# A hybrid decoder layer on one core: decode scores packed by sample, block scores in one product, values by mixed rows and triangles, and norm sums by 128 tokens

## The chip, the core and the metric

The kernel is one program on one core of a Trainium2 chip. Its engines work side by side, each through its own instructions in order: PE (TensorE, matrix products, with PEld for its weight loads), DVE (VectorE), ACT (ScalarE), POOL (GpSimd), and SP, which issues most transfers. Products go into one of eight banks of PSUM, each 512 float32 columns on 128 partitions, and DVE or ACT take them out from there. The metric is the device time of one execution in microseconds, the median of several runs.

## The reference

One step of a decoder layer in float32, for 1024 prompt tokens and 8 samples of 4 new tokens each (1056 tokens in all), width 1024. Cut to what the change touches:

```python
def _rms(x, g):
    y = xf * lax.rsqrt(jnp.mean(xf * xf, axis=-1, keepdims=True) + EPS)
    return y * g

def _sink_attention(q, k, v, mask, sinks):      # 8 heads of 64, 2 kv heads
    s = jnp.einsum('bnqhgd,bnkhd->bnhgqk', q, k) * (HEAD_DIM ** -0.5)
    s = jnp.where(mask, s, -jnp.inf)
    m = jnp.maximum(jnp.max(s, -1, keepdims=True), sink)
    p = jnp.exp(s - m)
    w = p / (jnp.sum(p, -1, keepdims=True) + jnp.exp(sink - m))
    return jnp.einsum('bnhgqk,bnkhd->bnqhgd', w, v)

def _layer(x, p, attn_fn, ...):
    h = _rms(x, n_mix_pre); z = h @ w_in         # q | k | v | u
    a = attn_fn(q, k, v)                         # prompt or sample
    m = pool_mixer(u)
    x = x + _rms(concatenate([a, m]) @ w_out, n_mix_post)
    f = _rms(x, n_ffn_pre)
    f = (silu(f @ w_gate) * (f @ w_up)) @ w_down
    x = x + _rms(f, n_ffn_post)
    return x + sigmoid(x @ w_ple_gate) * (p @ w_ple)
```

A prompt query attends to the 128 keys that end with its own: in blocks of 128 tokens these are the keys of its own block up to its place, and the keys of the block before it behind its place. A sample's query attends to the last 128 of 128 cached and 4 new keys of its own sample.

## The kernel before

**Tiling.** Activations lie with the width on partitions and tokens on columns, in three groups `g` of 352 tokens. Products of weights are made of two float32r halves of each operand (`wh`/`wl`, `mh`/`ml`, `fh`/`fl`): `gemm` issues three matmuls for each pair. ACT makes the high half by a copy and DVE the low half by a subtraction (`split`, lines 164 and 165). Attention's products (line 126, operands `a`), the transposes (line 120) and the norms' column sums are plain float32; one such product of float32 leaves two records in the trace, a transpose leaves one.

**Norms.** `rstd_steps` is a generator that the twelve norms of the kernel go through. The squares of a group stand in `acc`; four matmuls with `ones` give the sums of four times 88 tokens on 88 partitions, ACT and DVE take the root and its reciprocal (`sd`), split into two parts (`hl`). DVE multiplies each part into a diagonal (`dg`, two tiles of 88x352), and two matmuls with `ones_r` spread these over all partitions. A `yield` hands back to whatever is interleaved with the norm.

**Attention, decode.** `qd` holds the queries of 8 samples x 4 tokens x 4 heads, 128 in all, one kv head on each half of the partitions. `dscores(kv)` multiplies all of them with the keys of all samples (1024 cached and 32 new columns) and adds a mask that leaves each query its own sample's keys; `softmax` runs over 1056 columns, `dturned` transposes nine pieces, `dvalues` multiplies with the cached and new values.

**Attention, prompt.** The blocks run in the order 5, 6, 7, 0, 1, 2, 3, 4. `scores(b)` makes four heads x two kv heads x (own block, block before) products of 128 columns. ACT copies the part of the block before (line 678), DVE overwrites it with the own block's where the mask says so (line 679): a query's row then holds exactly its 128 keys. `softmax` reduces (DVE), exponentiates each head (ACT, line 642) and normalises (POOL, line 648). `turned` transposes the eight heads' weights; DVE multiplies each with two masks (lines 695 and 697), one result for the own block, one for the block before. `values` multiplies both with the values of the two blocks into one bank, and `put` splits the result into `mixa` (ACT line 627, DVE line 628).

**Order.** In this part PE's order is pinned to the order of the code. `filler(n)` takes the next output products (`out_pool`, `out_attn`, `out_proj`) from a list and puts them between the attention steps, so that PE has work while softmax and masks run on the others; what is left is issued behind the last block. The order on the other engines, outside what is pinned, comes from a scheduler. Tiles of activations share one pool with `A_SLOTS` places; a transfer into such a tile waits until its place is free.

Of the kernel before, what the change touches and what calls it, by code (L numbers as in the profile page):

```python
# [10 lines left out]
F32 = mybir.dt.float32  # L11
# [5 lines left out]
P = 128  # L17
D = 1024
# [11 lines left out]

TB = 4
WIN = 128
# [24 lines left out]

A_SLOTS = 27


@with_exitstack
def trunk_kernel(
# [61 lines left out]
    def mm(*args, **kw):  # L124

        ins = te.matmul(*args, **kw)  # L126
        if pinned[0]:
            tc.keep_in_program_order(ins)
# [4 lines left out]
    def tmp(n, s="t", dt=F32):  # L133
        return spool.tile([P, n], dt, tag="tmp", bufs=6, name=nm(s), padded_shape=[P, NX])
# [172 lines left out]
    def rstd_steps(acc):  # L307

        n = acc.shape[1]
        w = n // TB
# [4 lines left out]
        se.activation(sd[:w], sm[:w, :TB], AF.Sqrt, bias=epst[:w], scale=1.0 / D)  # L317
        ve.reciprocal(sd[:w], sd[:w])
        hl = spool.tile([P, 2, TB], F32R, tag="hl", name=nm("hl"))
        ve.tensor_copy(hl[:w, 0], sd[:w])  # L320
        ve.tensor_tensor(hl[:w, 1], sd[:w], hl[:w, 0].bitcast(F32), op=ALU.subtract)
        dgs = []
        for h in range(2):
            dg = tmp(n, "dg", F32R)
            ve.tensor_tensor(
                dg[:w].rearrange("p (i k) -> p i k", k=w),
                ident[:w, :w].unsqueeze(1).to_broadcast([w, TB, w]),
                hl[:w, h].bitcast(F32).unsqueeze(2).to_broadcast([w, TB, w]),
                op=ALU.mult,
            )  # L330
            dgs.append(dg)
# [229 lines left out]
    def u_mix(c):  # L561

        for g in range(G):
# [27 lines left out]
    misc = act_tile([P, 6, P])  # L591
    qd, am, vdec = misc[:, 0, :], misc[:, 1:5, :], misc[: NDEC * DSEQ, 5, :]
    for c in range(4):
        n = NDEC * DSEQ
        ge.tensor_copy(qd[:, c * n : (c + 1) * n], qT[c][:, SEQ:])
    ys = [[half(g, s="y"), None] for g in range(G)]
# [4 lines left out]

    vtok = act_tile([P, NB, P])
    for h in range(2):
        ps = bank()
        for i in range(4):
            b = 4 * h + i
            te.transpose(ps[:, i * P : (i + 1) * P], vT[:, b * P : (b + 1) * P], ident)
        se.copy(vtok[:, 4 * h : 4 * h + 4, :], ps.rearrange("p (b c) -> p b c", c=P))
    ps = bank()
# [39 lines left out]

    def m4(i):  # L650
        return am[:, i, :].unsqueeze(1).to_broadcast([P, 4, WIN])

# [3 lines left out]
    def scores(b):  # L656


        t = act_tile([P, 8, WIN])
        cur = [bank() for _ in range(2)]  # L660
        prv = [bank() for _ in range(2)] if b else None
        for c in range(4):
            for which, at in ((cur, b), (prv, b - 1)):
                if which is None:
                    continue
                for kv in range(2):
                    rows = slice(64 * kv, 64 * kv + 64)
                    mm(
                        which[kv][:, c * WIN : (c + 1) * WIN],
                        qT[c][rows, b * WIN : (b + 1) * WIN],  # L670
                        kT[rows, at * WIN : (at + 1) * WIN],
                        start=True,
                        stop=True,
                    )
        for kv in range(2):
            tk = t[:, 4 * kv : 4 * kv + 4, :]
            if b:
                se.copy(tk, v4(prv[kv]))
                ve.copy_predicated(tk, m4(0).bitcast(mybir.dt.int32), v4(cur[kv]))
            else:  # L680
                ve.tensor_tensor(tk, v4(cur[kv]), m4(1), op=ALU.add)
            hs = slice(4 * kv, 4 * kv + 4)
            softmax(tk, 4, 0.125, skp[:, hs], nskp[:, hs])
        return t

    def turned(b, t):

        ptc = act_tile([P, 8, WIN])
        ptp = act_tile([P, 8, WIN]) if b else None
        for kv in range(2):  # L690
            ps = bank()
            hs = slice(4 * kv, 4 * kv + 4)
            for c in range(4):
                mt(ps[:, c * P : (c + 1) * P], t[:, 4 * kv + c, :])
            ve.tensor_tensor(ptc[:, hs, :], v4(ps), m4(2), op=ALU.mult)
            if b:
                ve.tensor_tensor(ptp[:, hs, :], v4(ps), m4(3), op=ALU.mult)
        return [(ptc, b)] + ([(ptp, b - 1)] if b else [])

    def values(b, parts):  # L700
        o = bank()
        for n, (pt, at) in enumerate(parts):
            for kv in range(2):
                mm(
                    o[64 * kv : 64 * kv + 64, :],
                    vtok[:, at, 64 * kv : 64 * kv + 64],
                    pt[:, 4 * kv : 4 * kv + 4, :],
                    start=n == 0,
                    stop=n == len(parts) - 1,
                )  # L710
        put(o, b * WIN, WIN)


    ckt = act_tile([P, NDEC, WIN])
    cvt = act_tile([P, NDEC, P])
    dmt = act_tile([P, NDEC * WIN + NDEC * DSEQ])
    nc.sync.dma_start(ckt, ck)
    nc.sync.dma_start(cvt, cv)
    nc.sync.dma_start(dmt, dmask)
    NK = NDEC * WIN + NDEC * DSEQ  # L720

    def dscores(kv):
        rows = slice(64 * kv, 64 * kv + 64)
        q = qd[rows]
        t = act_tile([P, 1, NK])
        for lo, n in ((0, 512), (512, 512), (1024, NDEC * DSEQ)):
            ps = bank()
            if lo < 1024:
                k = ckt[rows].rearrange("p b w -> p (b w)")[:, lo : lo + n]
            else:  # L730
                k = kT[rows, SEQ:]
            mm(ps[:, :n], q, k, start=True, stop=True)
            ve.tensor_tensor(t[:, 0, lo : lo + n], ps[:, :n], dmt[:, lo : lo + n], op=ALU.add)
        softmax(t, 1, 0.125, skd[:, kv : kv + 1], nskd[:, kv : kv + 1])
        return t

    def dturned(t):
        pt = act_tile([P, NDEC + 1, P])
        for lo in (0, 4, 8):
            ps = bank()  # L740
            n = min(4, NDEC + 1 - lo)
            if lo < 8:
                for i in range(n):
                    mt(ps[:, i * P : (i + 1) * P], t[:, 0, (lo + i) * P : (lo + i + 1) * P])
                se.copy(pt[:, lo : lo + n, :], ps.rearrange("p (b c) -> p b c", c=P))
            else:
                mt(ps[: NDEC * DSEQ, :P], t[:, 0, 1024:])
                se.copy(pt[: NDEC * DSEQ, 8, :], ps[: NDEC * DSEQ, :P])
        return pt

    def dvalues(kv, pt, o):
        cols = slice(64 * kv, 64 * kv + 64)
        for b in range(NDEC):
            mm(o[cols, :P], cvt[:, b, cols], pt[:, b, :], start=b == 0, stop=False)
        mm(o[cols, :P], vdec[:, cols], pt[: NDEC * DSEQ, 8, :], start=False, stop=True)

# [51 lines left out]
    pinned[0] = True  # L808
    td = [dscores(kv) for kv in range(2)]
    t = scores(order[0])  # L810
    filler(2)
    od = bank()
    pt0 = dturned(td[0])
    filler(1)
    pt1 = dturned(td[1])
    dvalues(0, pt0, od)
    filler(1)
    dvalues(1, pt1, od)
    put(od, SEQ, NDEC * DSEQ)
# [436 lines left out]
def _layout(i):  # L1256
# [12 lines left out]
    q, c = np.arange(WIN)[:, None], np.arange(WIN)[None, :]  # L1269
    masks = np.stack([1.0 * (c <= q), np.where(c <= q, 0.0, NEG), 1.0 * (q <= c), 1.0 * (q > c)], 1)  # L1270
    r = np.arange(P)[:, None]
    rb, rj = (r % 32) // DSEQ, r % DSEQ
    kb, kw = np.arange(NDEC * WIN)[None, :] // WIN, np.arange(NDEC * WIN)[None, :] % WIN
    nb, nj = np.arange(NDEC * DSEQ)[None, :] // DSEQ, np.arange(NDEC * DSEQ)[None, :] % DSEQ
    dmask = np.concatenate([(rb == kb) & (kw > rj), (rb == nb) & (nj <= rj)], 1)
    pfix = np.stack([np.maximum(w / (np.arange(16) + 1.0), 1.0) for w in PW])
# [52 lines left out]
```

## Time and profile before

| | |
|---|---|
| median of 3 runs | 1134.02 us (1132.97 to 1134.21) |
| span of the profiled execution | 1132.5 us |
| granted TensorE clock, mean | 0.995 |
| PE busy | 1111.7 us, 98% of the span |
| DVE busy | 783.6 us, 69% |
| ACT busy | 454.3 us, 40% |
| POOL busy | 199.0 us, 18% |
| moved by DMA | 102.16 MB |

The profiled execution's own time is its span, from the first to the last instruction; the median of the runs is 1.5 us longer. In the trace the input products run to about 134 us, attention with its fillers from there to about 235, the rest of the output products, the feed-forward part and the per-layer input behind that. Times in the rows are in microseconds from the start of the span. In a row, `b<-a,a 128*64 128x512` is a matrix product into a bank from two activation tiles, with weights of 128 rows and 64 columns and 512 columns streamed; `c` is a constant.

### The profile page before, as it was taken

What the parts mean: (1) busy time and instruction counts of PE and PEld (TensorE: products, weight loads), DVE (VectorE), ACT (ScalarE), POOL (GpSimd) and SP (SyncE); (2) the same over time, 40 slices, a digit from 0 to 9 for tenths busy, and PEclk for the clock granted to TensorE, in tenths of its full rate; (3) what the DMA queues carried; (4) which work ended last, traced back from release to release, by engine and by line L of the source; (5) the groups of instructions that cost most, each with busy time, mean ns of one, the idle gap of its engine ahead of it and who ended that gap; (6) DMA issues with size and microseconds to landing.
All of it is one profiled execution on the core that took longest, in us unless ns stands there. A gap on an engine that the chain in (4) does not pass through costs nothing. (4 is left out here: it accounts for less than half of the span.)

```text
span 1132.5 us, 17606 instructions
## 1 busy us (share of the span) xinstructions
PE 1111.7 (98%) x7067; PEld 1087.4 (96%) x7067; DVE 783.6 (69%) x1283; ACT 454.3 (40%) x793; POOL 199.0 (18%) x165
## 2 busy tenths in 40 slices
PE   8999999999999999999999999999999999999797
PEld 8999987799999999999999999999999999999697
DVE  6666457876888965355554556547887877789786
ACT  7322266764555523331321313123424334364432
POOL 0044032200000042011111101111141132100231
PEclk9999999999999999999999999999999999999899
DMA  8121310172553312111110212122112222427041
GB/s 285 56 69 56 113 50 20 44 274 74 187 189 117 131 38 76 38 53 60 38 57 19 75 38 75 38 88 76 61 52 94 75 69 94 143 82 258 31 156 58
DMA packets 35985, 102.16 MB, mean 90 GB/s; under 512 B 4260, under 2 KB 14788, under 8 KB 35904
## 3 DMA queue, kind: packets, MB, share of 16 engines
q1 hardware_dynamic: 34576, 99.27, 25.8%
q10 hardware_dynamic: 1328, 1.77, 0.5%
q8 instruction: 55, 0.90, 0.3%
q14 instruction: 26, 0.21, 0.1%
HBM read 90.92 MB, written 10.11 MB: 89 GB/s over the span
## 5 line engine op out<-in xcount | busy, mean ns | idle before, releaser
L126 PE MATMUL b<-hid,wh 128*128 128x352 f32 x1056 | 252.7, 322 | 1.4 <-DVE o L1104 0.8
L164 ACT CAST wh<-wr 128x1024 fp32r<-128x1024 f32 (+1 forms) x135 | 138.4, 1029 | 249.3 <-PE b L126 205.6
L126 PE MATMUL b<-fh,wh 128*128 128x352 f32 x712 | 230.5, 324 | 0.0
L126 PE MATMUL b<-fl,wh 128*128 128x352 f32 x712 | 228.8, 321 | 0.0
L126 PE MATMUL b<-fh,wl 128*128 128x352 f32 x712 | 228.7, 321 | 0.0
L968 POOL TENSOR_TENSOR wr<-wr 128x512 f32<-128x512 f32 x52 | 74.3, 1428 | 738.7 <-DVE wl L165 451.9
L165 DVE TENSOR_TENSOR wl<-wr,wh 128x1024 fp32r<-128x1024 f32 (+1 forms) x135 | 165.4, 1229 | 40.2 <-ACT wh L164 39.9
L126 PEld LDWEIGHTS b<-hid,wh 128*128 128x128 f32 x1056 | 182.5, 188 | 2.2 <-PE b L126 1.1
L126 PE MATMUL b<-hid,wl 128*128 128x352 f32 x528 | 169.1, 320 | 0.0
L1065 DVE TENSOR_TENSOR o<-o,b 128x352 f32<-128x352 f32 x240 | 115.0, 514 | 29.5 <-PE b L126 29.4
L126 PEld LDWEIGHTS b<-fl,wh 128*128 128x128 f32 x712 | 134.4, 189 | 0.0
L126 PE MATMUL b<-fh,sh 128*128 128x352 f32 x416 | 134.3, 323 | 0.0
L126 PEld LDWEIGHTS b<-fh,wh 128*128 128x128 f32 x712 | 134.2, 188 | 0.0
L126 PEld LDWEIGHTS b<-fh,wl 128*128 128x128 f32 x712 | 134.1, 188 | 0.0
L126 PE MATMUL b<-fh,sl 128*128 128x352 f32 x416 | 133.5, 321 | 0.0
L126 PE MATMUL b<-fl,sh 128*128 128x352 f32 x416 | 133.3, 320 | 0.0
L165 DVE TENSOR_TENSOR sl<-wr,sh 128x1024 fp32r<-128x1024 f32 x52 | 63.5, 1222 | 84.5 <-ACT sh L164 84.5
L164 ACT CAST sh<-wr 128x1024 fp32r<-128x1024 f32 x52 | 53.9, 1047 | 144.4 <-POOL wr L968 104.8
L126 PE MATMUL b<-h,wh 128*128 128x352 f32 x480 | 105.8, 326 | 1.5 <-ACT h L379 1.1
L126 PEld LDWEIGHTS b<-hid,wl 128*128 128x128 f32 x528 | 98.9, 187 | 0.0
L126 PEld LDWEIGHTS b<-h,wh 128*128 128x128 f32 x480 | 82.5, 190 | 2.4 <-ACT h L379 1.3
L126 PEld LDWEIGHTS b<-fl,sh 128*128 128x128 f32 x416 | 78.3, 188 | 0.0
(175 smaller groups left out, 1695.4 us busy)
## 6 DMA issues: line engine op xcount, KB each, us to landing
wr<-in_w_gu_dram SPq DMA_DIRECT2D x64, 512.0 KB, 3.3
wr<-in_w_dn_dram SPq DMA_DIRECT2D x32, 512.0 KB, 3.3
wr<-in_w_pg_dram SPq DMA_DIRECT2D x18, 512.0 KB, 3.5
x<-in_x_dram SPq DMA_DIRECT2D x6, 704.0 KB, 10.6
x1d<-x SPq DMA_DIRECT2D x6, 704.0 KB, 3.6
x<-x1d SPq DMA_DIRECT2D x6, 704.0 KB, 5.5
out_y_dram<-yo SPq DMA_DIRECT2D x24, 176.0 KB, 1.9
wr<-in_w_out_b_dram SPq DMA_DIRECT2D x8, 512.0 KB, 4.2
```

The lines of the kernel that those rows point to most:

```text
L126: ins = te.matmul(*args, **kw)
L164: fix(se.copy(hi, src))
L165: fix(ve.tensor_tensor(lo, src, hi.bitcast(F32), op=ALU.subtract))
L968: ge.tensor_tensor(out, a, b, op=op)
L1065: ve.tensor_tensor(o, o, v, op=ALU.add)
```

## The change

Five things change at once.

1. `TB` goes from 4 to 3: a norm's sums are made for three times 128 tokens (the last two overlap, 352 = 128 + 128 + 96), and `dg` is one tile [128, 2, 352] that two DVE multiplies fill, one of 2 x 256 columns and one of 2 x 96.
2. Decode: the queries are also laid out in `qm`, one matrix of 128 columns for each sample that is zero but for that sample's queries; `dscores` accumulates the eight samples' products into the same 128 columns, so the scores are 160 columns a kv head (128 cached, 32 new), both heads go through one softmax, four transposes take the place of eighteen, and `dvalues` multiplies 16 columns at a time for each sample and head. The transposed weights are copied out by ACT once.
3. `scores(b)` takes the keys of the block before and the own block in one product of 256 columns. The evictions (ACT copy, DVE masked copy) become four of 256 columns each where there were two of 512.
4. `values` of a block that has a block before it: `vmix` holds, on partitions 0 to 63, the first 64 values of the block itself and, on 64 to 127, the last 64 of the block before. Every query uses at least some of each of these halves, and one product with 128 rows takes them for each half of the queries; the remaining two triangles of 64 keys are products on 64 rows. Two banks hold the two halves of the queries, so `put` runs twice with 64 tokens. Block 0 has no mask product: ACT copies the transposed weights.
5. `A_SLOTS` goes to 28, the scratch of dynamic transfers is set to 1024, and decode uses three fillers instead of four, so one more output product is left for later.

```diff
-TB = 4
+TB = 3
-A_SLOTS = 27
+A_SLOTS = 28
 # rstd_steps
-        for i in range(TB):
-            mm(sm[:w, i : i + 1], acc[:, i * w : (i + 1) * w], ones[:, 0:1], start=True, stop=True)
+        for i, lo in enumerate((0, P, n - P)):
+            mm(sm[:, i : i + 1], acc[:, lo : lo + P], ones[:, 0:1], start=True, stop=True)
-        for h in range(2):
-            dg = tmp(n, "dg", F32R)
-            ve.tensor_tensor(dg[:w]..., ident[:w, :w]..., hl[:w, h]..., op=ALU.mult)
+        dg = spool.tile([P, 2, n], F32R, tag="dg", name=nm("dg"))
+        ve.tensor_tensor(dg[:, :, : 2 * P]..., ident..., f[:, :, 0:2]..., op=ALU.mult)
+        ve.tensor_tensor(dg[:, :, 2 * P :], ident[:, P - rest :]..., f[:, :, 2:3]..., op=ALU.mult)
         yield 6, 14
-            mm(ps[:, :n], ones_r[:w, :], dgs[h][:w], start=h == 0, stop=h == 1)
+            mm(ps[:, :n], ones_r, dg[:, h], start=h == 0, stop=h == 1)
 # queries and values
+    qm = act_tile([P, NDEC * P + 4 * NDEC * DSEQ], s="qm")
+    ge.memset(qm, 0.0)
+        ge.tensor_copy(own[:, :, :DSEQ], new.rearrange("p (b j) -> p b j", j=DSEQ))
+        se.copy(vmix[0:64, 4 * h : 4 * h + 4, :], four[0:64])
+        se.copy(vmix[64:P, 4 * h + 1 : 4 * h + 1 + n, :], four[64:P, :n])
 # scores
+                mm(both[kv][c // per][:, at : at + w * WIN], qT[c][rows, b * WIN : (b + 1) * WIN],
+                    kT[rows, first : first + w * WIN], start=True, stop=True)
-                se.copy(tk, v4(prv[kv]))
-                ve.copy_predicated(tk, m4(0).bitcast(mybir.dt.int32), v4(cur[kv]))
+                for i in range(2):
+                    se.copy(th, two[:, :, 0, :])
+                    ve.copy_predicated(th, m4(0, 2).bitcast(mybir.dt.int32), two[:, :, 1, :])
 # turned
             if b:
+                ve.tensor_tensor(ptx[:, hs, :], v4(ps), m4(2), op=ALU.mult)
+                ve.tensor_tensor(pty[:, hs, :], v4(ps), m4(3), op=ALU.mult)
+            else:
+                se.copy(ptx[:, hs, :], v4(ps))
 # values
+        for cols, hs in heads:
+            for o, qs in zip(os2, halves):
+                mm(o[cols, :256], vmix[:, b, cols], ptx[:, hs, qs], start=True, stop=False)
+        for kv, (cols, hs) in enumerate(heads):
+            for i in range(2):
+                lo = (i + kv) % 2
+                qs = halves[lo]
+                mm(os2[lo][cols, :256], vtok[qs, b - 1 + lo, cols], pty[qs, hs, qs], start=False, stop=True)
+        for o, qs in zip(os2, halves):
+            put(o, b * WIN + qs.start, 64)
 # decode
+        for b in range(NDEC):
+            for _, rows, ps in kvs:
+                mm(ps[:, :WIN], qm[rows, b * P : (b + 1) * P], ckt[rows, b, :], start=b == 0, stop=b == NDEC - 1)
+        softmax(t, 2, 0.125, skd, nskd)
+        se.copy(pt[:, 0:2, :], two[:, 0:2, :])
+        se.copy(pt[: NDEC * DSEQ, 2:4, :], two[: NDEC * DSEQ, 2:4, :])
-    td = [dscores(kv) for kv in range(2)]
+    td = dscores()
     t = scores(order[0])
     filler(2)
-    od = bank()
-    pt0 = dturned(td[0])
-    filler(1)
-    pt1 = dturned(td[1])
-    dvalues(0, pt0, od)
+    ptd = dturned(td)
     filler(1)
-    dvalues(1, pt1, od)
+    od = bank()
+    dvalues(ptd, od)
     put(od, SEQ, NDEC * DSEQ)
```

The order of DVE's instructions at the first norm, before:

```order
L320 CAST hl_319<-sd_316 88x4
L321 TENSOR_TENSOR hl_319<-sd_316,hl_319 88x4
L325 TENSOR_TENSOR dg_322<-c_77,hl_319 88x352
L325 TENSOR_TENSOR dg_324<-c_77,hl_319 88x352
L344 TENSOR_TENSOR xr_114<-xr_114,xr_118 128x1408
```

And with the change (line 349 is the addition of line 344, for the next group's squares):

```order
L320 CAST hl_318<-sd_315 128x3
L321 TENSOR_TENSOR hl_318<-sd_315,hl_318 128x3
L349 TENSOR_TENSOR xr_114<-xr_114,xr_118 128x1408
L325 TENSOR_TENSOR dg_321<-c_77,hl_318 128x2x256
L331 TENSOR_TENSOR dg_321<-c_77,hl_318 128x2x96
```

The 1408-wide addition moved from behind the two multiplies of `dg` to ahead of them.

The order of ACT's instructions at the decode part, before; `a_1349` and `a_1371` are the decode scores, `a_1393` block 5's, `a_1477` the first head's transposed weights:

```order
L642 ACTIVATE a_1371,sm_1388<-a_1371,nmx_1383 128x1056
L678 COPY a_1393<-b_1396 128x512
L678 COPY a_1393<-b_1397 128x512
L764 COPY y_1316<-b_1448 128x352
L764 COPY y_1314<-b_1462 128x352
L745 COPY a_1477<-b_1478 128x512
L745 COPY a_1477<-b_1484 128x512
L748 COPY a_1477<-b_1490 32x128
L764 COPY y_1315<-b_1493 128x352
L639 ACTIVATE es_1420<-es_1420 128x4
L642 ACTIVATE a_1393,sm_1423<-a_1393,nmx_1418 128x128 x4
```

With the change, `a_1390` are block 5's scores and `a_1469` the transposed decode weights:

```order
L696 COPY a_1390<-b_1394 128x256
L797 COPY y_1316<-b_1441 128x352
L657 ACTIVATE a_1390,sm_1414<-a_1390,nmx_1409 128x128 x2
L654 ACTIVATE es_1411<-es_1411 128x4
L657 ACTIVATE a_1390,sm_1414<-a_1390,nmx_1409 128x128 x2
L654 ACTIVATE es_1430<-es_1430 128x4
L657 ACTIVATE a_1390,sm_1433<-a_1390,nmx_1428 128x128 x4
L797 COPY y_1314<-b_1455 128x352
L771 COPY a_1469<-b_1470 128x256
L772 COPY a_1469<-b_1470 32x256
```

The copies of the transposed decode weights (745 and 748 before, 771 and 772 now) stand behind block 5's eight exponentials instead of ahead of them.

Block 0's transposed weights, `a_1944`, on DVE before, amid block 1's maxima:

```order
L634 TENSOR_REDUCE mx_1915<-a_1875 128x4
L636 SCALAR_TENSOR_TENSOR nmx_1900<-mx_1898,c_1318 128x4
L695 TENSOR_TENSOR a_1944<-b_1945,a_1309 128x512
L638 TENSOR_TENSOR es_1902<-c_75,nmx_1900 128x4
L636 SCALAR_TENSOR_TENSOR nmx_1917<-mx_1915,c_1318 128x4
L695 TENSOR_TENSOR a_1944<-b_1951,a_1309 128x512
```

With the change on ACT, `a_1906`:

```order
L657 ACTIVATE a_1841,sm_1865<-a_1841,nmx_1860 128x128 x3
L654 ACTIVATE es_1881<-es_1881 128x4
L657 ACTIVATE a_1841,sm_1884<-a_1841,nmx_1879 128x128 x4
L717 COPY a_1906<-b_1907 128x512
L717 COPY a_1906<-b_1913 128x512
```

They moved from DVE to ACT, behind the exponentials of block 1 (`a_1841`).

More of the change, by code (lines that the diff above doesn't have):

```diff
@@ L659, in scores @@
         t = act_tile([P, 8, WIN])
-        cur = [bank() for _ in range(2)]
-        prv = [bank() for _ in range(2)] if b else None
+        w = 2 if b else 1
+        first = (b - w + 1) * WIN
+        per = 4 // w
+        both = [[bank() for _ in range(w)] for _ in range(2)]
         for c in range(4):
[L663 to L674, printed above, removed]
+            for kv in range(2):
+                rows = slice(64 * kv, 64 * kv + 64)
+                at = (c % per) * w * WIN
+                mm(
+                    both[kv][c // per][:, at : at + w * WIN],
+                    qT[c][rows, b * WIN : (b + 1) * WIN],
+                    kT[rows, first : first + w * WIN],
+                    start=True,
+                    stop=True,
+                )
         for kv in range(2):
@@ L719, in trunk_kernel, with dscores @@
     nc.sync.dma_start(dmt, dmask)
[L720 to L734, printed above, removed]
+    def dscores():
+        t = act_tile([P, 2, NK])
+        kvs = [(kv, slice(64 * kv, 64 * kv + 64), bank()) for kv in range(2)]
+        for b in range(NDEC):
+            for _, rows, ps in kvs:
+                mm(ps[:, :WIN], qm[rows, b * P : (b + 1) * P], ckt[rows, b, :], start=b == 0, stop=b == NDEC - 1)
+        for _, rows, ps in kvs:
+            mm(ps[:, WIN:NK], qd[rows], kT[rows, SEQ:], start=True, stop=True)
+        for kv, _, ps in kvs:
+            ve.tensor_tensor(t[:, kv, :], ps[:, :NK], dmt[:, kv, :], op=ALU.add)
+        softmax(t, 2, 0.125, skd, nskd)
@@ new lines, in dturned, with dvalues @@
+        two = ps.rearrange("p (k r) -> p k r", r=P)
+        se.copy(pt[:, 0:2, :], two[:, 0:2, :])
+        se.copy(pt[: NDEC * DSEQ, 2:4, :], two[: NDEC * DSEQ, 2:4, :])
+        return pt
+    def dvalues(pt, o):
+        heads = [slice(64 * kv, 64 * kv + 64) for kv in range(2)]
+        for kv, cols in enumerate(heads):
+            mm(o[cols, :P], vdec[:, cols], pt[: NDEC * DSEQ, 2 + kv, :], start=True, stop=False)
+        by_b = lambda a: a.rearrange("p (c b j) -> p c b j", c=4, j=DSEQ)
+        for b in range(NDEC):
+            for kv, cols in enumerate(heads):
+                mm(
+                    by_b(o[cols, :P])[:, :, b, :],
+                    cvt[:, b, cols],
+                    by_b(pt[:, kv, :])[:, :, b, :],
+                    start=False,
+                    stop=b == NDEC - 1,
+                )
```

113 lines of the change are left out of this document (57 added, 56 removed).

## The prediction

> **What bounds the kernel now.** I read the page's busy times first, then the span, PE's list of waits, and busy time by stage.
>
> ```profile
> PE 1111.7 (98%) x7067; PEld 1087.4 (96%) x7067; DVE 783.6 (69%) x1283; ACT 454.3 (40%) x793; POOL 199.0 (18%) x165
> core 0: 1132.5 us, clock 0.995
> ```
>
> PE (TensorE) is busy for 98% of the span, so time is saved only where PE has fewer or shorter passes or where one of its few stalls goes. The span of the profiled execution is 1132.5 us and the median of the runs 1134.0: 1.5 us lie outside the span, and I add every change to 1134.0.
>
> ```profile
> PE b L126 <- ACT p L1196: 5.9, 1, 5.9
> PE b L126 <- DVE dg L325: 1.2, 2, 0.8
> ...
> PE b L126 <- DVE a L695: 0.8, 3, 0.4
> PE b L126 <- DVE es L638: 0.8, 1, 0.8
> ```
>
> Columns: who waited, for whom, us in total, how often, the longest. PE's largest wait (5.9 us) is near the end. Of the others the change touches the broadcast of a norm (dg, 1.2 us) and the attention blocks (L695 and L638, 0.8 us each).
>
> ```profile
> 192.00:225.00 33.00, 31.42 (x211) 23.60 (x210) 28.77 (x66) 23.71 (x81) 6.54 (x7) 1.00 0.15 49
> 225.00:240.00 15.00, 15.00 (x97) 13.37 (x97) 8.96 (x15) 7.07 (x12) 0.00 (x0) 1.00 0.94 319
> 240.00:1005.00 765.00, 763.59 (x4818) 762.73 (x4817) 519.29 (x808) 282.50 (x405) 122.64 (x88) 1.00 0.24 82
> 1005.00:1067.00 62.00, 54.58 (x342) 52.96 (x340) 58.37 (x84) 33.38 (x43) 0.63 (x1) 0.99 0.41 141
> ```
>
> After the length stand busy PE, PEld, DVE, ACT and POOL, clock, DMA share, GB/s. From 240 to 1005 PE idles for 1.4 us in 765: whatever the attention gives or takes before 240 is carried through. From 1005 to 1067 DVE (VectorE) is the bound (58.4 of 62), and the 5.9 us wait lies there. Its DVE work stays the same but for one norm's multiplies, so that stretch starts earlier or later as a whole and I count 0 for it.
>
> **Norms.** The first norm beside the input products, all engines:
>
> ```profile
> 23.92 0.71 PE L126 MATMUL b<-c,acc 128*88 128x1 f32 x8
> ...
> 26.72 0.16 DVE L321 TENSOR_TENSOR hl<-sd,hl 88x4 fp32r<-88x4 f32 x1
> 26.81 0.94 DVE L325 TENSOR_TENSOR dg<-c,hl 88x352 fp32r<-88x352 f32 x2
> ...
> 27.47 0.77 PE L126 MATMUL b<-dg,c 88*128 88x352 f32 x2 [0.81 <-DVE dg L325]
> 27.68 1.61 DVE L344 TENSOR_TENSOR xr<-xr,xr 128x1408 f32<-128x1408 f32 x1
> ```
>
> PE waits here for dg. In the new order the 1408-wide addition stands between hl and the two multiplies of dg. dg is then complete one addition later, and the second broadcast, which before could trail the first, now needs both parts as the first does. I count the 1.61 us of the addition: **+1.6** (1.3 to 2.1). Behind the stalled broadcast PE's queue holds the key products, so nothing fills the gap. The multiplies themselves stay two instructions over 704 columns together (2 x 352, now 2 x 256 and 2 x 96), within 0.1 us. For the sums, 8 passes (0.71 us with the last one's tail, hence some 0.07 us each) become 6 with 128 instead of 88 weight columns. If a pass follows the weight width, 6 x 0.07 x 128/88 is 0.6 us against 0.6: nothing; from -0.14 to +0.1 us a norm at the ends, ±1 us over twelve. The other eleven broadcasts together waited 0.4 us.
>
> **Decode.** PE, in order of time:
>
> ```profile
> 134.90 4.96 PE L126 MATMUL b<-a,a 64*128 64x512 f32 x44
> 144.34 1.20 PE L120 MATMUL b<-c,a 128*128 128x128 f32 x9 [0.42 <-POOL a L648]
> ...
> 147.30 1.14 PE L120 MATMUL b<-c,a 128*128 128x128 f32 x9
> 148.38 2.32 PE L126 MATMUL b<-a,a 128*64 128x128 f32 x18
> ...
> 152.73 4.30 PE L126 MATMUL b<-a,a 128*64 128x128 f32 x50
> ```
>
> A matrix product in f32 leaves two records (passes), a transpose one. The last row holds 18 passes of decode values and the 32 passes of the next block's scores, so scores take 4.30 - 2.32 = 1.98 us, and the first row, less its 32 passes of scores, gives 4.96 - 1.98 = 2.98 us for the decode scores.
>
> - Scores: now 32 passes of 128 columns on alternating row halves, the shape of a block's scores (1.98 us), and two 32-column products (0.1): 2.1, hence -0.9. Their padded queries are filled by POOL copies, and the last stands behind the copy that before ended the preparation:
>
> ```profile
> 134.61 0.21 POOL L595 COPY a<-a 128x32 f32<-128x32 f32 x1 [12.65 <-DVE a L580]
> ```
>
>   It ended at 134.82, just ahead of PE's 134.90. One more copy costs about 0.25. Together **-0.6** (-1.0 to 0). The zeroing of the padded queries runs long before, on an idle POOL.
> - Transposes: 18 passes in 1.20 + 1.14 us are 0.13 each; 4 cost 0.53. The wait of 0.42 goes too, since the softmax is 320 wide instead of 2112: **-2.2** (-2.4 to -1.8).
> - Values: 2 x 2.32 us become 32 passes of 16 columns and 4 of 128. No row has 16 columns. With 0.07 us a pass, the one-column row, they take 2.8 us in a single stream, and half of that if the two column halves run side by side as the halves of a block do. I take the middle, 2.1: **-2.5** (-3.2 to -1.8). The Trainium skill (TensorEngine Tiling (Array Packing), Instruction Overhead) puts a product of one column at the price of one of 60, about 60 cycles; at 2.4 GHz, the full clock in the opening table of its TensorE: Matmul & The Clock Gate, that is by estimate 25 ns; the 32 passes would take 0.8 us and the term would be -3.3. The trace disagrees: its one-column passes take 0.07 us, nearly three times that.
> - A new wait. ACT (ScalarE) copies the transposed decode weights for PE:
>
> ```profile
> 143.21 1.05 ACT L678 COPY a<-b 128x512 f32<-128x512 f32 x2
> ...
> 147.96 0.39 ACT L642 ACTIVATE a<-a,nmx 128x128 f32<-128x128 f32 x1
> ...
> 151.13 1.04 ACT L745 COPY a<-b 128x512 f32<-128x512 f32 x2
> ```
>
>   Before, the first set of copies stood ahead of block 5's eight exponentials; now the only set stands behind them, and those take 151.13 - 147.96 = 3.2 us from the first. PE's sequence to decode values is then 135.15 + 2.1 + 2.0 + two fillers (3.9) + 0.5 + a filler (1.9) = 145.6. Block 5's evictions (L678) began at 143.21, behind the decode exponentials, and its own exponentials 4.75 us after that. With a decode softmax of 320 columns instead of 2112 the evictions can begin once block 5's scores are done, at 135.15 + 2.1 + 2.0 = 139.3 and a little; the exponentials then begin near 144.2. They end at 147.4, and the two copies make it 148.1. PE waits 2.5 us, and behind the values in its queue are block 6's scores: **+2.5** (0.5 to 4.5).
>
> (A filler is one output product of 12 matmuls, 1.93 us; the decode part uses three instead of four, and the fourth runs later, so this moves PE work without changing it.)
>
> **Prompt blocks.** Scores: 8 products of 256 columns in the place of 16 of 128, the same columns. Fewer gaps: 0.07 us a block, **-0.5** (-1.2 to 0). Values of a masked block (block 3), DVE and then PE:
>
> ```profile
> 222.55 0.68 DVE L697 TENSOR_TENSOR a<-b,a 128x512 f32<-128x512 f32 x1
> ```
>
> ```profile
> 222.69 1.93 PE L126 MATMUL b<-a,a 128*64 128x512 f32 x6 [0.21 <-DVE a L695]
> ```
>
> DVE's last mask multiply ends at 223.23, and values end at 224.62, 1.4 us later, because 512-column passes over both parts still follow. Now the mixed product of that head needs only the multiply before (L695's), and behind the last multiply remain two triangles of 256 columns on 64 rows, in different quarters of the array: about 0.9 us. That is 0.5 less in each of 7 blocks: **-3.5** (-5 to 0). The waits L695 and L638 of the earlier list, 1.6 us, lie at the same place; DVE's order there no longer puts a weight split ahead of the next block's evictions: **-1.6** (-2.3 to 0).
>
> Block 0 has no masked part. Its multiply on DVE (its last one in the first row below) becomes a plain copy on ACT (block 1's first exponential and the instruction behind the last):
>
> ```profile
> 187.70 0.68 DVE L695 TENSOR_TENSOR a<-b,a 128x512 f32<-128x512 f32 x1
> ```
>
> ```profile
> 187.13 0.40 ACT L642 ACTIVATE a<-a,nmx 128x128 f32<-128x128 f32 x1 [0.74 <-DVE nmx L636]
> ...
> 190.41 0.43 ACT L764 COPY y<-b 128x352 f32<-128x352 f32 x1
> ```
>
> DVE had it ready at 188.38, amid block 1's exponentials. ACT's two copies now stand behind those, so they start at 190.41 and end near 191.4: 3 us later, of which I leave half a microsecond to the shorter evictions ahead: **+2.5** (0 to 4.5). Behind block 0's values on PE stand block 2's scores, so no later block makes up for it.
>
> Covered: the four extra copies for the mixed rows, on ACT before the decode exponentials, which wait for DVE. The x loads on SP now stand ahead of the last two blocks of output weights instead of one; 0, unless the transfers of 225 to 240 (share 0.94) become the bound, a rival below.
>
> **The sum.** -0.6 - 2.2 - 2.5 + 2.5 - 0.5 - 3.5 - 1.6 + 2.5 = -5.9 in attention, +1.6 in the first norm: -4.3, so 1134.0 becomes **1129.7 us**.
>
> **Rivals.**
>
> *DVE becomes the bound of every masked block (slower).* Splitting a 512-column instruction costs its fixed part once more:
>
> ```profile
> L628 DVE TENSOR_TENSOR ml<-b,mh 128x512 fp32r<-128x512 f32 x6 | 4.1, 687 | 1.3 <-ACT mh L627 1.3
> L628 DVE TENSOR_TENSOR ml<-b,mh 128x256 fp32r<-128x256 f32 x2 | 0.8, 417 | 0.0
> ```
>
> 2 x 417 - 687 = 147 ns. Each masked block has two more masked evictions and one more split of its result on DVE, 0.44 us, over 7 blocks +3.1. DVE was already busy for 28.8 of 33 us at 192 to 225. If each block lasts as long as its DVE work, the -3.5 and -1.6 go, and +3.1 comes: -4.3 + 8.2 = +3.9, **1137.9**. It decides where the DVE work of a block exceeds PE's products and fillers. Against it: L695 and L638 together held PE for only 1.6 us.
>
> *The gain is swallowed (no change).* If the x loads or the first gate and up weights, in the stretch with DMA at 0.94, arrive no sooner, PE waits at about 240 for what it gained: **1134.0**. For it: that stretch is full. Against: the loads start when attention's tiles come free, so they move along, and PE is busy for all of 225 to 240.
>
> *The clock drops.* After the 5.9 us wait:
>
> ```profile
> 1061.00 0.32 PE L126 MATMUL b<-fl,wh 128*128 128x352 f32 x1
> 1061.16 0.32 PE L126 MATMUL b<-fh,wl 128*128 128x352 f32 x1
> ...
> 1069.28 0.49 PE L126 MATMUL b<-fh,wh 128*128 128x352 f32 x1
> 1069.57 0.49 PE L126 MATMUL b<-fl,wh 128*128 128x352 f32 x1
> ```
>
> Starts lie 0.29 us apart instead of 0.16. If each new wait of about 2.5 us does that to 12 matmuls, it is 1.6 us twice: -4.3 + 3.2 = -1.1, **1132.9**. PE's list has no wait between 1.2 and 5.9 us, so no row decides it. The Trainium skill (TensorE: Matmul & The Clock Gate, Part 1) gives a free-running activity window of about 3.4 us; by that rule waits of 2.5 us should leave the clock up, and it speaks against this rival.
>
> *More is saved.* ACT's copies come sooner than I work out (the new waits 0.5 and 0 instead of 2.5 each): -8.8, **1125.2**.
>
> **How the numbers follow.** Forecast 0.50, DVE-bound blocks 0.13, swallowed 0.15, clock 0.12, more saved 0.10. The unknown terms of the forecast (decode values ±0.7, the waits ±2, masked values +3.5 to -1.5, norms ±1) spread it by some 4 us. The range 1125.0 to 1136.0 leaves out DVE-bound blocks and the far end of the good case. About 0.2% (2.3 us) can be told from no change: faster, below 1131.7, has nearly all of the forecast and the good case, 0.60; same has the swallowed and the clock case, 0.25; slower 0.15.
>
> **What would show it.** Right: the first norm's broadcast on PE waits for dg by about 2.4 us; one wait of 2 to 3 us for the ACT copy of decode weights; another for ACT's copy of block 0; PE's first sums after attention, before at 237, come about 4 us earlier; 240 to 1005 keeps its length. Wrong: waits of half a microsecond or more for L697, L714 or L715 (DVE) in most blocks; a masked block's values ending 1.4 us behind the last multiply as before; PE idle on DMA near 240; a lower clock at 30 or 148.

## The result, and the profile after

| | before | after |
|---|---|---|
| median | 1134.14 us (1132.97 to 1136.34, 20 runs) | 1135.95 us (1133.52 to 1139.19, 20 runs) |
| span of the profiled execution | 1132.5 us | 1133.3 us |
| PE busy | 1111.7 us | 1105.8 us |
| mean clock | 0.995 | 0.991 |

The ratio is 1.0016, with a 95% interval of 1.0008 to 1.0024: the kernel became 1.8 us slower, where 4.3 us less were forecast. (The spans differ by 0.8 us only: the profiled execution of the changed kernel took 1135.13 us, less than the median.) Ratios leave out three slow executions of later kernels, one of 1352 us at a clock of 0.75 and two of 2197 us. PE has less to do, and it waits more. First its waits after the change:

```profile
PE b L126 <- ACT p L1226: 4.7, 1, 4.7
PE b L126 <- DVE dg L331: 3.8, 3, 2.3
PE b L126 <- ACT a L772: 2.8, 1, 2.8
...
PE b L126 <- ACT a L717: 1.5, 1, 1.5
```

L331 is a norm's broadcast, L772 the copy of the decode weights, L717 block 0's copy on ACT: the three waits that were forecast. The first two have the size that was forecast (2.4 and 2.5 us); the third is smaller (2.5). So far attention and the first norm do what they should. The timeline of PE at the sums of the first norm behind attention, before and then after:

```profile
237.16 0.71 PE L126 MATMUL b<-c,acc 128*88 128x1 f32 x8
```

```profile
232.49 0.83 PE L126 MATMUL b<-c,acc 128*128 128x1 f32 x6 [0.77 <-DVE acc L807]
```

At this place PE is 4.67 us ahead, with 1.5 us of the first norm's wait in it. The same comparison further on, at the ninth norm's broadcast, the sums of the tenth, and its broadcast, first before:

```profile
356.71 0.49 PE L126 MATMUL b<-dg,c 88*128 88x352 f32 x2
...
798.43 0.71 PE L126 MATMUL b<-c,acc 128*88 128x1 f32 x8
...
1010.42 0.86 PE L126 MATMUL b<-dg,c 88*128 88x352 f32 x2 [0.38 <-DVE dg L325]
```

and after:

```profile
352.40 0.48 PE L126 MATMUL b<-dg,c 128*128 128x352 f32 x2
...
797.21 0.72 PE L126 MATMUL b<-c,acc 128*128 128x1 f32 x6
...
1010.31 0.59 PE L126 MATMUL b<-dg,c 128*128 128x352 f32 x2 [1.23 <-DVE dg L331]
```

The lead is 4.3 us at 356, 1.2 at 798 and 0.1 at 1010 (the last broadcast named is the eleventh's). Most of it goes between 356 and 798, where PE never stops, on the same instructions. The busy time by stage for 400 to 780 us, before and after, shows it in the count of products behind PE's busy time:

```profile
400.00:780.00 380.00, 380.00 (x2393) 380.00 (x2392) 203.77 (x336) 107.97 (x166) 69.39 (x52) 1.00 0.16 54
```

```profile
400.00:780.00 380.00, 380.00 (x2377) 380.00 (x2376) 204.29 (x337) 107.96 (x165) 65.43 (x50) 1.00 0.17 54
```

Both are at a granted clock of 1.00 and have no idle time, and yet one makes 2393 products in 380 us and the other 2377: 158.9 against 160.0 ns from the start of one product of 352 columns to the start of the next. From 356 to 798 us that is 3 us. This spacing is called the pace below.

### The profile page after: what moved, and what is told of

Its sections match the earlier page's. It is cut to its first block, busy times and chain, and to the rows that moved or that the text cites. A ratio compares the mean times of both kernels' runs of the same rounds, so it can differ in the third digit from the quotient of the medians.

```text
span 1133.3 us, 17508 instructions
## 1 busy us (share of the span) xinstructions
PE 1105.8 (98%) x6997; PEld 1086.1 (96%) x6997; DVE 778.2 (69%) x1292; ACT 456.0 (40%) x814; POOL 200.6 (18%) x169
## 5 line engine op out<-in xcount | busy, mean ns | idle before, releaser
L126 PEld LDWEIGHTS b<-fh,sl 128*128 128x128 f32 x416 | 78.5, 189 | 0.0
```

## The experiments

Two theories stood at first: the new norms set this pace, or each execution draws it. A third had the loss in the DVE-bound stretch behind 1005 us.

**The change once more, and its two halves.** First the kernel itself (no edit).

> The changed kernel once more, unchanged. Two theories on where the 4.7 us that attention had gained by 232 us went between 240 and 820 us, where PE is busy without a break in both kernels. Pace: the spacing of the 352-column products there is one of a few fixed values (158.9 ns before, 160.0 ns after), and the new shape of the norms' passes sets a slower one; then 400 to 780 us shows 160.0 ns or slower again. Chance: the value is drawn anew in each execution whatever the kernel; then a second profile may as well show 158.9, and the median comes near 1134.

Measured: 1136.89 us, ratio 1.0020 (1.0011 to 1.0029), and in this stretch the pace of the first profile, so it is not drawn anew by each execution as far as two profiles show:

```profile
400.00:780.00 380.00, 380.00 (x2377) 380.00 (x2377) 202.96 (x334) 106.11 (x163) 68.70 (x52) 1.00 0.16 54
```

Then the attention alone, with the norms of before:

```diff
-TB = 3
+TB = 4
 # rstd_steps: the text of the kernel before
```

> The changed kernel with the norms of before (4 x 88 sums, two dg tiles). Pace theory: 158.9 ns at 400 to 780 us; the first norm's wait falls back to 0.8 us; the sums behind attention come some 6 us earlier than in the kernel before, and the time is 1128 to 1130 us. Chance theory: spacing and spread as in the changed kernel; only the 1.5 us of the first norm come back, about 1134.4. Tail theory (the loss is in the DVE-bound stretch from 1005 us, because of the norms' other order there): 1134 to 1132.5 us with that stretch as long as before.

Measured: 1128.06 us, ratio 0.9952 (0.9940 to 0.9965). The pace is that of the kernel before:

```profile
400.00:780.00 380.00, 380.00 (x2394) 380.00 (x2392) 209.43 (x346) 107.94 (x166) 64.10 (x48) 1.00 0.16 56
```

And the norms alone, in the kernel before:

```diff
-TB = 4
+TB = 3
 # rstd_steps: the text of the changed kernel
+    nc = _bacc.Bacc(..., dynamic_dma_scratch_size=1024)
```

> The kernel before with the new norms alone (and the smaller scratch of transfers, without which they do not fit). Pace theory: 160.0 ns or slower at 400 to 780 us and +1.5 us at the first norm, 1138 to 1141 us. Chance theory: +1.5 us only, 1135.7 us. Tail theory: +1.5 us and 1 to 2 us more behind 1005 us, 1137 us.

Measured: 1141.93 us, ratio 1.0064 (1.0052 to 1.0076), so +7.6 us, 0.9 us above the range that the pace theory gave. Its waits and its pace:

```profile
PE b L126 <- DVE dg L331: 4.4, 3, 3.0
```

```profile
400.00:780.00 380.00, 380.00 (x2377) 380.00 (x2377) 204.69 (x333) 106.82 (x164) 68.71 (x50) 1.00 0.16 54
```

Against the kernel before as measured beside them (1134.29 us), attention is worth 6.2 us and the norms cost 7.6 us. By the ratios that is 0.48% less and 0.64% more, together the 0.16% of the whole change. The tail theory falls: with the norms alone, the way from the eleventh broadcast to the 5.9 us wait is not longer than before.

**The three waits.** The copies of the decode weights and of block 0 go to DVE, and the first norm's multiplies are placed ahead of the long addition:

```diff
-        se.copy(pt[:, 0:2, :], two[:, 0:2, :])
-        se.copy(pt[: NDEC * DSEQ, 2:4, :], two[: NDEC * DSEQ, 2:4, :])
+        ve.tensor_copy(pt[:, 0:2, :], two[:, 0:2, :])
+        ve.tensor_copy(pt[: NDEC * DSEQ, 2:4, :], two[: NDEC * DSEQ, 2:4, :])
-                se.copy(ptx[:, hs, :], v4(ps))
+                ve.tensor_copy(ptx[:, hs, :], v4(ps))
+            tc.add_manual_dep(first.ins, last_dg[0].ins.name, ...)   # sum_halves behind dg
```

> The changed kernel with the three instructions that PE waited for moved: decode weights and block 0's weights copied out by DVE instead of ACT, and the first norm's dg multiplies ahead of the 1408-wide addition. All theories: waits of 2.3, 2.8 and 1.5 us shrink to 0.8, under 0.5 and under 0.5, the clock stays at 1.00 at 150 us (it fell to 0.86 there), and the sums behind attention come 6 to 8 us earlier than in the changed kernel (about 225 to 227 us). Pace theory: spacing of 160.0 ns or slower at 400 to 780 us, about 1130 us. If DVE were the bound in the blocks, the copies would only move the waits and the time would stay near 1135.9.

Measured: 1132.10 us, ratio 0.9976 (0.9967 to 0.9985), 2377 products at 400 to 780 us. Block 0's wait is gone. The first norm's is shorter, but 1.6 us instead of the 0.8 expected. The one at the decode values stays, the clock falls behind it (0.51 at 153 to 157 us), and the sums behind attention start at 231.3 us, not at 225 to 227:

```profile
PE b L126 <- DVE dg L333: 3.0, 3, 1.6
PE b L126 <- ACT y L807: 2.6, 1, 2.6
```

PE now waits as long for another ACT instruction (the last eviction of a filler, L807), so the copy's own place behind the exponentials was not the whole cause: ACT is late as a whole. The timeline of ACT in the changed kernel shows a reason:

```profile
137.03 0.58 ACT L621 COPY a<-b 64x512 f32<-64x512 f32 x1
137.62 0.58 ACT L623 COPY a<-b 64x512 f32<-64x512 f32 x1
...
138.70 0.58 ACT L621 COPY a<-b 64x512 f32<-64x512 f32 x1
...
139.29 0.47 ACT L623 COPY a<-b 64x384 f32<-64x384 f32 x1
...
141.06 1.28 ACT L657 ACT_TABLE_LOAD   x1 [1.02 <-issue]
142.36 0.43 ACT L657 ACTIVATE a<-a,nmx 128x160 f32<-128x160 f32 x1
```

Before, the table load stood here:

```profile
137.44 1.28 ACT L642 ACT_TABLE_LOAD   x1 [1.41 <-issue]
```

The four copies for the mixed rows (2.2 us) stand ahead of it, and everything behind it on ACT is later. (Of the 3.6 us between the two loads, 1.7 are there already when ACT begins to copy the values, at 136.55 against 134.82.) So POOL copies these rows, in the kernel with the old norms, and nothing else is changed:

```diff
-        se.copy(vmix[0:64, 4 * h : 4 * h + 4, :], four[0:64])
-        se.copy(vmix[64:P, 4 * h + 1 : 4 * h + 1 + n, :], four[64:P, :n])
+        ge.tensor_copy(vmix[0:64, 4 * h : 4 * h + 4, :], vtok[0:64, 4 * h : 4 * h + 4, :])
+        ge.tensor_copy(vmix[64:P, 4 * h + 1 : 4 * h + 1 + n, :], vtok[64:P, 4 * h : 4 * h + n, :])
```

> The kernel with the changed attention and the norms of before, with one edit: the rows for the mixed values copied by POOL instead of ACT. If ACT's four extra copies are what makes the decode part late (the table load came at 141.1 us instead of 137.4): the exponentials of block 5 begin 2 to 2.3 us earlier, the wait of 2.8 us at decode values falls to 0.5 to 0.9 us, the clock stays up there, and the time is 1124 to 1126 us. If only the order on ACT counts: 1128 us still.

Measured: 1125.63 us, ratio 0.9915 (0.9898 to 0.9932). That is 2.4 us less than with the old norms alone, or 3.8 if each is set against the kernel before as measured beside it (1135.64 and 1134.29 us). Counted from ACT's first copy of the values, block 5's exponentials begin 7.3 us later instead of 9.3, so the 2 us earlier that were expected. The wait at the decode values is 1.0 us, a little more than expected, and the clock stays up at that place:

```profile
PE b L126 <- ACT a L767: 1.0, 1, 1.0
```

```profile
144.00:154.00 10.00, 9.04 (x89) 8.04 (x88) 4.61 (x17) 6.46 (x28) 3.19 (x4) 1.00 0.23 89
```

Last, these edits at attention together on the old norms, with the evictions of the first three fillers on DVE too:

```diff
-        se.copy(ys[g][0][:, m, :], ps[:, : NS[g]])
+        (se.copy if m else ve.tensor_copy)(ys[g][0][:, m, :], ps[:, : NS[g]])
```

> The changed attention with the norms of before, and the order mended: the rows for the mixed values copied by POOL instead of ACT, decode weights, block 0's weights and the first three output products taken out by DVE instead of ACT. All theories: the waits of 2.8 us at decode values and of 1.5 us at block 0 fall under 1 us each, the clock stays at 1.00 at 150 us, and with the spacing of 158.9 ns the time is 4 to 6 us below the 1128.1 us of the kernel with the old norms alone: 1122 to 1124.5. If DVE cannot take the copies: no faster than 1127.

Measured: **1121.27 us, ratio 0.9886 (0.9872 to 0.9900)**: some 13 us below the kernel before, and below what was expected. What each edit gives in it was not tried one by one. PE has no wait left in the decode part:

```profile
140.00:160.00 20.00, 20.00 (x169) 17.41 (x168) 15.22 (x49) 12.29 (x54) 5.96 (x7) 1.00 0.14 51
```

**What in the norms sets the pace.** The new norms differ in the rows of the broadcast, the passes of the sums, their width, and in `dg`. First the rows, in the kernel with the old norms:

```diff
+        ve.memset(sd, 1.0)
-            mm(ps[:, :n], ones_r[:w, :], dgs[h][:w], start=h == 0, stop=h == 1)
+            mm(ps[:, :n], ones_r, dgs[h], start=h == 0, stop=h == 1)   # rows 88 to 127 zero
```

> The changed kernel with the norms of before (four sums of 88, two dg tiles), but the broadcast of each norm made with all 128 rows (rows 88 to 127 of dg are zero). If the broadcast's rows set the pace: the spacing behind the last broadcast ahead of the long stretch (about 350 us) goes to 160.0 ns, as with the new norms, and the time is about 1131.5 us. If the shape of the sums sets it: 158.9 ns to 790 us and 1128 us as without this edit.

Measured: 1128.26 us, 2394 products at 400 to 780 us. Not the rows. Then a fourth sum in the changed kernel:

```diff
-        for i, lo in enumerate(at):
+        for i, lo in enumerate(at + (P,)):
```

> The changed kernel with a fourth sum of 128 tokens in each norm (its result is not used), so that the sums are 8 passes again as in the kernel before. If the number of passes sets the pace: 158.9 ns at 400 to 780 us and about 1134 us. If the broadcast's rows or the sums' width set it: 160.0 ns still, and 12 x 0.22 = 2.6 us more at most, 1136 to 1139 us.

Measured: 1137.63 us, 2377 products. Not the number of passes. Then `dg` in two tiles in the changed kernel:

```diff
-        dg = spool.tile([P, 2, n], F32R, tag="dg", name=nm("dg"))
+        for h in range(2):
+            dg = tmp(n, "dg", F32R)    # two multiplies for each
```

> The changed kernel with its new norms, but dg as two tiles from the shared pool as in the kernel before (four multiplies, two of 256 and two of 96 columns). If the single dg tile is what leaves the slower pace: 158.9 ns at 400 to 780 us, and with the multiplies ahead of the 1408-wide addition 1131 us or a little less. If the sums of 128 tokens do: 160.0 ns, about 1134.

Measured: 1131.46 us, with all sums still of 128 tokens, and

```profile
400.00:780.00 380.00, 380.00 (x2394) 380.00 (x2393) 207.63 (x344) 109.10 (x166) 65.22 (x49) 1.00 0.16 56
```

(The waits for dg fall too, to 1.5 us in all, so the time isn't the pace's alone.) And the converse, one tile for the old norms:

```diff
+        dgt = spool.tile([P, 2, n], F32R, tag="dg", name=nm("dg"))
-            dg = tmp(n, "dg", F32R)
+            dg = dgt[:, h]
```

> The changed kernel with the norms of before, but both parts of dg in one tile of its own. If the single dg tile leaves the slower pace: 160.0 ns at 400 to 780 us and about 1131.3 us. If the sums of 128 tokens do: 158.9 ns and 1128 us as with the old norms.

Measured: 1132.60 us, 4.5 us more than with two tiles, or 2.6 by the ratios (0.9975 and 0.9952). Again, for the profile:

> The norms of before with both parts of dg in one tile, once more for its profile (the first one was taken at a clock of 0.75). If the single dg tile leaves the slower pace: 160.0 ns at 400 to 780 us. If not, its 4 us over the kernel with two tiles come from elsewhere, and the spacing is 158.9 ns.

Measured: 1133.09 us, and this pace:

```profile
400.00:780.00 380.00, 380.00 (x2377) 380.00 (x2376) 204.91 (x337) 107.67 (x165) 65.55 (x49) 1.00 0.16 55
```

So in this stretch the pace goes with the tile, with old sums or new: 2377 with a single one, 2394 with two. Is it that there is one tile, or where its halves lie?

```diff
-        dg = spool.tile([P, 2, n], F32R, tag="dg", name=nm("dg"))
+        dg = spool.tile([P, 2, 512], F32R, tag="dg", bufs=1, name=nm("dg"))[:, :, :n]
```

> The changed kernel with the two parts of the single dg tile 512 columns apart instead of 352 (one such tile instead of two in turn). If the distance of the two parts in memory sets the pace: 158.9 ns at 400 to 780 us and about 1133 us. If it is the single tile in any form (that both broadcasts come ready at once, say): 160.0 ns and about 1136.

Measured: 1135.15 us, and

```profile
400.00:780.00 380.00, 380.00 (x2394) 380.00 (x2393) 203.75 (x336) 107.89 (x166) 69.66 (x52) 1.00 0.16 54
```

One tile with its halves further apart leaves the faster pace, so it isn't the number of tiles. (Its single buffer changes the moments of the passes as well.) The time gains little, and the 1133 us expected were missed. The profile is of the slowest of the ten runs (1138.04 us): there the waits for dg are 5.5 us in all against 3.8, the clock is 0.50 from 876.5 to 879.9 us behind a wait of 2.0 us, and 885 to 990 us has 653 products against 663 in the changed kernel. Whether this is what the other runs lost isn't shown.

Last, whether the pace is left behind by what PE did at the broadcast: one product more there, in the changed kernel, with `dg` as it is.

```diff
+        if turn_no in (8,):
+            mm(ps[:, 400:401], acc[:, :P], ones[:, 0:1], start=True, stop=True)
```

> The changed kernel with one product more: a column sum of the usual shape (128x128, one column, result not used) directly behind the ninth norm's broadcast, the last one ahead of the long stretch. If the pace is a state that the passes of a norm leave behind and that then lasts: in the profile of the changed kernel the sums at 343 us were followed by 158.9 ns, so the stretch to 790 us runs at 158.9 instead of 160.0 ns, 0.7% of some 435 us, and the time falls by about 3 us less the 0.3 us that it costs, to 1133 us. If the pace belongs to the program's layout of memory: 160.0 ns and 0.3 us more, about 1136.5 us.

Measured: 1134.22 us, ratio 0.9995 (0.9986 to 1.0004), 1.7 to 2.7 us less than the two measurements of the changed kernel:

```profile
400.00:780.00 380.00, 380.00 (x2393) 380.00 (x2392) 204.37 (x336) 107.71 (x165) 68.55 (x52) 1.00 0.16 54
```

One useless product, and 440 us behind it run faster. (Behind a later wait this kernel is slower: 653 products at 885 to 990 us against 663.)

Other stretches of the same profiles say more on place and moment. The changed kernel in its first and its second profile, between two waits for DVE:

```profile
833.00:872.00 39.00, 39.00 (x247) 39.00 (x246) 27.84 (x44) 14.95 (x21) 11.07 (x8) 1.00 0.21 68
```

```profile
833.00:872.00 39.00, 39.00 (x244) 39.00 (x244) 31.06 (x50) 14.79 (x20) 9.42 (x7) 1.00 0.23 80
```

It is the same program with the same layout, and it runs at 158.9 ns once and at 161.1 ns the other time. So the layout alone doesn't fix the pace. And behind the second of these waits, a kernel with two tiles (POOL copying the rows) and then one with a single tile:

```profile
885.00:990.00 105.00, 105.00 (x654) 105.00 (x653) 77.73 (x120) 42.64 (x58) 22.63 (x17) 1.00 0.31 107
```

```profile
885.00:990.00 105.00, 105.00 (x663) 105.00 (x662) 79.54 (x125) 40.60 (x56) 27.62 (x20) 1.00 0.28 99
```

Here the two tiles go with the slower pace. A single tile isn't slow in itself: it leaves the slower pace at the ninth norm's broadcast, where PE comes in without a wait and the changed kernel shows the same in both profiles. That the longest stretch of the kernel, 440 us, stands behind this broadcast is bad luck.

## Why the prediction was wrong, by its own steps

- **"Whatever the attention gives or takes before 240 is carried through"** is the step that failed. It took PE's time for a product as fixed while PE is busy. It isn't: of the 4.67 us lead, 3 were lost between 356 and 798 us without a wait, on 2778 products of the same shape in both kernels. The prediction's own sign, that 240 to 1005 keeps its length, failed.
- **The norms** were sized at +1.6 us for the first and 0 for the other eleven. The first was right (wait 0.81 to 2.34 us, and the addition stood ahead of dg as told). The zero was wrong: the others cost through the pace (3 us) and at the eleventh broadcast (0.38 to 1.23 us; three other instructions of DVE stand between the reciprocal and dg there, where there were two). The norms alone cost 7.6 us. Their profile accounts for 6.2 of it: 1.9 at the first norm, 3.1 in the long stretch, 0.9 at the eleventh broadcast, the rest in small parts. The other four runs were 1.3 to 1.6 us longer at a lower mean clock (0.993 to 0.995 against 0.996), and no profile shows why.
- **Attention** was right in sum: -5.9 forecast, 4.67 + 1.5 = 6.2 us found at 232 us, and 6.2 us in the time with the old norms. In part this is luck, for its terms missed both ways. The masked blocks' values, with the waits L695 and L638, gave 7.3 us instead of 5.1 (from start to start on PE 17.6 to 11.9 us in seven blocks, and 1.6 us of waits gone). Against that, the blocks' scores took 0.5 us more instead of 0.5 less, some of them at half the clock, and the first sums behind attention wait 0.8 us for their accumulation, which no term had. The wait for the decode copy was 2.8 us (2.5 forecast), but block 5's exponentials began at 145.8 instead of 144.2, in part since the four copies "covered" on ACT weren't covered. Block 0 waited 1.5 us on PE, its values took 0.5 us longer, and so it cost 2.0 in all (2.5 forecast).
- **Decode values:** the 32 passes of 16 columns took 1.04 us where the clock was full, 33 ns each, against 70 ns (single stream) or 35 ns (column halves side by side) by the prediction's row of one-column passes. So its lower end was right, and the middle that it took too high. The Trainium skill's price (TensorEngine Tiling (Array Packing), Instruction Overhead), by estimate 25 ns, was lower than the trace by a quarter.
- **The rival with the clock** came true at the decode wait. Busy time by stage in the changed kernel, and in the kernel with one product more, where the first row is behind the first norm's wait and the last behind the decode wait:

```profile
148.00:157.00 9.00, 6.91 (x64) 5.85 (x65) 2.85 (x9) 3.94 (x16) 3.18 (x4) 0.81 0.18 69
```

```profile
30.00:33.00 3.00, 3.00 (x12) 3.00 (x12) 3.00 (x8) 1.74 (x6) 0.00 (x0) 0.53 0.00 0
...
153.00:157.00 4.00, 4.00 (x34) 3.44 (x34) 0.84 (x3) 0.91 (x3) 0.67 (x2) 0.50 0.33 131
```

  A clock of 0.81 over 9 us is 1.7 us of lost work. Behind the first norm's wait it went either way: at 2.3 us in the first profile and at 3.0 us with the norms alone the clock stayed at 1.00, and at 2.7 to 3.0 us in three others it fell to between 0.50 and 0.63. In three more, the second profile of the changed kernel among them, it fell already behind a wait of 1.6 to 1.8 us for the sums' operand just before. That may be one source of the wider spread of the changed kernel's runs; it was not tried by itself. The prediction gave this rival 0.12 and leaned on the Trainium skill's window of 3.4 us (TensorE: Matmul & The Clock Gate, Part 1), by which shorter waits should leave the clock up: the trace disagrees, at the decode values waits of 2.6 to 3.2 us brought it down in each of the ten profiles that have one, and the wait of 1.0 us did not.
- **DVE as the bound of the blocks** did not come true. A masked block's values in the changed kernel, on DVE and on PE:

```profile
213.44 0.68 DVE L715 TENSOR_TENSOR a<-b,a 128x512 f32<-128x512 f32 x1
```

```profile
213.77 1.68 PE L126 MATMUL b<-a,a 128*64 128x256 f32 x16
```

  The multiply ends at 214.12 and the values at 215.45, 1.3 us behind it. By the prediction's own sign (1.4 us behind the multiply, as before) the -3.5 did not come the way it was told, through a shorter path behind the last multiply. It came because PE's own work in a masked block is shorter, here 1.6 us from start to start, and no wait for L714 or L715 is among PE's.

The profiled execution of the changed kernel lost 0.9 us more between the eleventh broadcast and 1068 us. ACT waits there for the load of the per-layer input, before and then after:

```profile
1048.80 0.49 ACT L164 CAST pl<-pr 128x352 fp32r<-128x352 f32 x1 [6.58 <-DMA pr<-in_p_dram]
```

```profile
1049.62 0.49 ACT L164 CAST pl<-pr 128x352 fp32r<-128x352 f32 x1 [8.26 <-DMA pr<-in_p_dram]
```

The transfer was issued 0.9 us earlier (1042.31 against 1043.20) and yet ended later, and DVE, the bound there, waited for it. Other profiles with the same norms lost nothing there, so this belongs to the one execution.

What stays open: why PE runs at one of several paces at all, and how a layout of `dg` brings about the other one. One product more changes the pace with the layout kept, and a wait changes it with the program kept, so it doesn't take another layout; that the moment is what counts, and that the layout acts through it, isn't shown.

## What to carry to other kernels

When PE is the bound and a profile shows no waits, count products per stretch, before and after: a pace that differs by 0.7% over hundreds of microseconds outweighs a handful of saved passes. Time a change's parts by themselves before sizing them together, for here one part gave 6.2 us and another took 7.6. And an instruction that is counted as covered by another engine's wait has to be followed to what stands behind it in its own queue: without four copies of 0.5 us on ACT, a wait on PE fell from 2.8 to 1.0 us and the clock stayed up behind it.

## What the hardware showed that was not expected

- With the clock at 1.00 and no idle time, the same products of 352 columns run over long stretches at one of three spacings: 158.9, 160.0 or 161.1 ns from start to start (2394 or 2377 in 380 us, 653 in 105 us). A spacing lasts for up to hundreds of microseconds; in these profiles it changed at a norm's passes and behind waits. In the stretch from 400 to 780 us it was the same in both profiles of the changed kernel and changed with the layout of an operand of the passes ahead (two tiles, one, one with its halves apart) and with one product more beside them. Behind a wait the same program showed 158.9 ns in one execution and 161.1 in another.
- One product more, with a result that nobody uses, shortened the time by about 2 us (1134.22 us against 1135.95 and 1136.89 us).
- Single waits of 2.6 to 3.2 us in an otherwise busy stream brought the granted clock down to 0.50 for some microseconds (0.81 over 9 us in the first profile); one of 1.0 us did not.
